# Attention's step list extended over the first two rows of its output product

## The chip, the cores and the metric

The kernel runs on one core of one Trainium2 chip. The metric is the device time of one execution in microseconds (us); before the change the median of three runs is 2084.99 us (2084.24 to 2086.21).

## The reference

Two layers work on x, 1024 tokens by 1024 features in float32. Layer 0 is a gated short convolution and a squared-ReLU MLP; layer 1 is latent attention with shared keys and values and the same kind of MLP. Around each stands a norm, a modulation and a gated sum. The change lies at the end of layer 1's attention:

```python
def mla_mixer(h, q_a_w, q_a_norm_g, q_b_w, o_w, k_nope, v, k_pe, cos, sin):
    q = (rmsnorm(h @ q_a_w, q_a_norm_g) @ q_b_w).reshape(B, S, N_HEADS, QK_NOPE + QK_ROPE)
    ...
    for i in range(S // Q_BLOCK):
        s = (jnp.einsum("bqhd,bkhd->bhqk", qn, k_nope[:, :k_end])
             + jnp.einsum("bqhr,bkr->bhqk", qp, k_pe[:, :k_end])).astype(jnp.float32)
        s = jnp.where(mask[None, None], s, jnp.finfo(jnp.float32).min)
        p = jax.nn.softmax(s, axis=-1).astype(v.dtype)
        outs.append(jnp.einsum("bhqk,bkhd->bqhd", p, v[:, :k_end]))
    o = jnp.concatenate(outs, axis=1).reshape(B, S, N_HEADS * V_HEAD)
    return o @ o_w
```

There are 8 heads of 128 value features. The last line, `o @ o_w`, is the output product: 1024 by 1024 times 1024 by 1024.

## The kernel before

**Precision.** Every large product is made of three matmuls of split operands: a value is kept as a high part (fp32r) and a low part (the rest), and `mm` (L225 to L227) issues low x high, high x low, high x high. The split costs one ScalarE instruction for the high part (L230) and one VectorE instruction for the low part (L231).

**The output product.** `down` (L906) works in rows. Row r holds 128 features of `o` (head r, stored in DRAM as `hd[r]`) and the 128 matching rows of `attn_o_w`, each split into high and low: one `slot` of four 128x1024 pieces. `fill_row` (L802) loads the two raw tiles on SyncE's queue (`ld`, L196) and makes the four pieces: two instructions on ScalarE (L230) and two on VectorE (L231). For each of 8 tiles of 128 tokens, a group of rows is multiplied into a PSUM tile `big` of two banks, of which there are two: 12 matmuls of 512 columns for a group of two rows. The groups are 2, 2 and 4 rows. For the first group ScalarE copies `big` into `y` (L941), for the second VectorE adds it (L943), and the last goes through the norm of the seam.

**Memory.** The raw tiles are a ring of four, shared by all loads. Attention keeps the queries and the rotary keys in slots 0 and 1; slot 2 has held an operand of the stage before and is not used in attention. The pool `pp` holds the shared keys and a cosine table. Before the change all this is released after attention, and six new slots are laid out (`arena_pool`) for the output product.

**Order.** The string `ATTENTION` is a list of steps. `pinned` records each step's instructions so that every engine keeps them in the list's order; SyncE's loads are pinned for the part that belongs to attention. The framework may still place instructions that are outside the list between them. The step names that matter here, for head h: S (scores into `big`), m (maximum, VectorE), e (exponential, ScalarE), t (scaling by the sum, VectorE); for a half of the queries and a group of key tiles: T (transposes into a `tp` PSUM tile), u and w (its high part on ScalarE, L1668, and its low part on VectorE, L1672, both into `pt`), P (product with the values), o (copy out, and store into `hd`). K, Q, R, V are the projections. bl and bs are loads and sums of a modulation vector that fill gaps.

```python
    for name in ATTENTION[n:]:
        acts[name]()
    ...
    at.release()
    tb.release()
    pp.release()
    ar[1].release()
    ...
    ar, slots = arena_pool()
    up, ws, hs, firsts, _ = down_phase(slots, (2, 2, 4), attn_o_w[0], from_dram(hd), "g1m", xs[1], xs[2], ...)
```

Of the kernel before, what the change touches and what calls it, by code (L numbers as in the profile page):

```python
# [66 lines left out]
mm5 mm6 add5 sq5 stt5 xad5 tr0_0 tr0_1 tu0_0 add6 mm7 dma5 tu0_1 rc4 sp0_0 sq6 sp0_1 sqx5 stt6 pre4 rc5 xad6 pre5 tr0_2 f0  # L67
add7 tu0_2 dma6 mul7 sqx6 tr0_3 tr0_4 sp0_2 f1 tu0_3 rc6 sq7 sp0_3 tr0_5 pre6 f2 stt7 tu0_5 tu0_4 sp0_5 dma7 tr0_6 tr0_7
sqx7 sp0_4 f3 tu0_6 rc7 pre7 sp0_6 f4 tu0_7 sp0_7 tr1_0 tr1_1 tu1_0 f5 tu1_1 sp1_0 sp1_1 tr1_2 tr1_3 tu1_2 f6 tu1_3 sp1_2
sp1_3 tr1_4 tr1_5 tu1_4 f7 tu1_5 sp1_4 sp1_5 tr1_6 qh00 tr1_7 g0 qh01 ql00 tu1_7 ql01 tu1_6 sp1_7 qq00 trk0_0 qh02 trk0_1  # L70
sp1_6 g1 tuk0_0 qq01 ql02 tuk0_1 qa01 trk0_2 spk0_0 trk0_3 qq02 g2 spk0_1 tuk0_3 qa02 tuk0_2 spk0_3 trk0_4 trk0_5 qs0 spk0_2
tuk0_5 g3 qr0 spk0_5 tuk0_4 spk0_4 e0 qi0 trk0_6 wa0 trk0_7 e2 qh10 wd0 qq10 tuk0_7 ql10 tuk0_6 spk0_7 trk1_0 qh12 trk1_1 e1
spk0_6 wa2 tuk1_1 ql12 tuk1_0 wd2 trk1_2 spk1_1 qq11 trk1_3 v00 wa1 qa11 tuk1_2 spk1_0 qq12 qh11 spk1_2 tuk1_3 qa12 spk1_3
ql11 trk1_4 wd1 vr00 trk1_5 qs1 tuk1_4 qwa trk1_6 spk1_4 k0 qr1 tuk1_6 qi1 qwd vq00 tuk1_5 spk1_6 spk1_5 trk1_7 v01 kwa
tuk1_7 kwd ka0 spk1_7 kz0 ky0 v11 ks0 vr01 kh0 vq01 kl0 va0 vs0 v10 vt0 vi0 vb0 vr10 k1 vn01 vr11 vn00 vq10 vq11 vh01 va1
vh00 vl01 vl00 vs1 ka1 bB0 R0.1 vt1 kz1 K0.0 Ra0.1 bl0.1 vi1 ky1 bl0.0 vb1 ks1 Q0.1 vn10 lq1 Ka0.0 vn11 vh10 Rz0.1 vh11
Kd0.0 Qa0.1 vl10 K1.0 kh1 Qd0.1 kl1 Q0.0 vl11 Ka1.0 qa1 Ry0.1 Kd1.0 Rs0.1 K0.1 Qa0.0 qd1 Rh0.1.0 Qd0.0 Rh0.1.1 R0.0 Rl0.1.0
Ka0.1 Rl0.1.1 Kd0.1 V0.3 bs0.0 Ra0.0 bs0.1 S0.7 bl0.2 Va0.3 bl0.3 Ry0.0 Rz0.0 S0.4 Vd0.3 Rs0.0 m0.7 V0.2 Rh0.0.0 Rh0.0.1
bs0.2 Q1.1 e0.7 Rl0.0.1 bl0.4 Va0.2 m0.4 S0.5 Qa1.1 t0.7 e0.4 Vd0.2 S0.6 Qd1.1 Rl0.0.0 m0.5 V0.0 m0.6 e0.5 V0.1 Va0.0 t0.4
e0.6 t0.5 S0.1 Vd0.0 Va0.1 S0.2 t0.6 K1.1 m0.1 Vd0.1 e0.1 T0.1.0 m0.2 T0.1.1 Ka1.1 S0.0 u0.1.0 t0.1 Q1.0 u0.1.1 lq2 Kd1.1  # L80
e0.2 w0.1.0 w0.1.1 lk1 T0.1.2 t0.2 Qa1.0 T0.1.3 m0.0 S0.3 u0.1.2 Qd1.0 u0.1.3 e0.0 w0.1.2 P0.1.0 qa2 w0.1.3 P0.1.1 t0.0
T0.1.4 qd2 P0.1.2 u0.1.4 m0.3 S1.4 xa1 w0.1.4 e0.3 xd1 R1.1 m1.4 t0.3 P0.1.3 e1.4 bs0.3 P0.1.4 Ra1.1 T0.1.5 t1.4 T0.1.6
bl0.5 S1.5 bs0.4 u0.1.6 Rz1.1 S1.7 u0.1.5 bl0.6 w0.1.6 w0.1.5 Ry1.1 m1.5 T0.0.0 Q2.1 u0.0.0 m1.7 e1.5 S1.6 w0.0.0 Qa2.1
Rs1.1 e1.7 Qd2.1 bs0.5 Rh1.1.0 T0.0.1 P0.1.5 Rh1.1.1 m1.6 u0.0.1 P0.1.6 bl0.7 P0.0.0 o0.1 T0.0.2 w0.0.1 S1.1 u0.0.2 t1.5
e1.6 K2.0 t1.7 P0.0.1 t1.6 Ka2.0 S1.2 w0.0.2 Kd2.0 P0.0.2 Rl1.1.0 T1.1.0 o0.0 T1.1.1 m1.2 V1.1 u1.1.1 Rl1.1.1 e1.2 w1.1.1
K2.1 u1.1.0 bs0.6 Va1.1 T1.1.2 w1.1.0 Ka2.1 S1.3 u1.1.2 Vd1.1 Kd2.1 T1.1.3 Q2.0 m1.3 u1.1.3 w1.1.3 e1.3 w1.1.2 R1.0 t1.2
Qa2.0 t1.3 Qd2.0 S1.0 bs0.7 Ra1.0 P1.1.0 lq3 P1.1.1 m1.0 m1.1 T1.1.4 T1.1.5 e1.0 P1.1.2 Rz1.0 u1.1.4 P1.1.3 Ry1.0 u1.1.5
w1.1.4 e1.1 S2.4 w1.1.5 qa3 Rs1.0 T1.1.6 qd3 P1.1.4 Rh1.0.1 t1.1 S2.7 Rh1.0.0 m2.4 u1.1.6 Rl1.0.1 e2.4 w1.1.6 t1.0 P1.1.5
m2.7 P1.1.6 Q3.1 o1.1 t2.4 e2.7 Rl1.0.0 S2.6 Qa3.1 t2.7 Qd3.1 K3.1 m2.6 V1.3 Ka3.1 e2.6 Kd3.1 T1.0.0 T1.0.1 Va1.3 t2.6 V1.2
u1.0.0 u1.0.1 Vd1.3 w1.0.0 S2.1 Va1.2 w1.0.1 V1.0 m2.1 Vd1.2 T1.0.2 e2.1 S2.5 u1.0.2 t2.1 Va1.0 w1.0.2 Vd1.0 S2.3 m2.5 bE0  # L90
m2.3 e2.5 e2.3 t2.5 S2.2 t2.3 bB1 bl1.0 bF0 T2.1.0 bl1.1 S2.0 u2.1.0 m2.2 lk2 P1.0.0 lq4 m2.0 P1.0.1 e2.2 w2.1.0 e2.0 P1.0.2
t2.2 T2.1.1 o1.0 K3.0 t2.0 bs1.0 u2.1.1 Q3.0 w2.1.1 Ka3.0 bl1.2 xa2 bs1.1 T2.1.2 Kd3.0 qa4 bl1.3 T2.1.3 xd2 P2.1.0 u2.1.2
# [24 lines left out]
u6.0.1 P6.0.0 t7.6 u6.0.2 e7.0 S7.3 w6.0.1 o6.1 w6.0.2 T7.1.0 t7.0 T7.1.1 m7.3 u7.1.0 P6.0.1 u7.1.1 w7.1.0 S7.1 e7.3 w7.1.1
P6.0.2 T7.1.2 m7.1 o6.0 T7.1.3 P7.1.0 t7.3 u7.1.3 P7.1.1 u7.1.2 w7.1.3 S7.2 e7.1 w7.1.2 T7.1.4 t7.1 T7.1.5 m7.2 u7.1.4
P7.1.2 u7.1.5 w7.1.4 P7.1.3 e7.2 w7.1.5 T7.1.6 P7.1.4 t7.2 u7.1.6 P7.1.5 w7.1.6 T7.0.0 T7.0.1 u7.0.0 P7.1.6 u7.0.1 w7.0.0
o7.1 w7.0.1 T7.0.2 P7.0.0 u7.0.2 P7.0.1 w7.0.2 P7.0.2 o7.0  # L120
""".split()

VEC_ROWS = 109
BIAS_ROWS = 112
C_ID, C_T = 0, 128
WIDE = 64
C_COLS = 2176


@with_exitstack  # L130
def trunk_kernel(ctx: ExitStack, tc: tile.TileContext, x, ada_w, ada_b, norm_g, conv_in_w, conv_out_w, kv_ada_w,
# [676 lines left out]
    def down_pairs(ys, wd, before):  # L808
# [1056 lines left out]
```

## Time and profile before

| | |
|---|---|
| median of three runs | 2084.99 us |
| the profiled execution | 2085.6 us, of which the span on the core is 2083.8 us |
| granted TensorE clock, mean of the span | 0.998 |
| busy share: PE, PE weight load, VectorE, ScalarE | 99%, 82%, 73%, 51% |
| stretch of the latents, from their first steps to the first head | about 997 to 1092 us |
| stretch of attention's heads | about 1092 to 1365 us |
| stretch of the output product's first two groups and of its last group up to the first transposes for the MLP | about 1365 to 1440 us |

PE is TensorE's matmuls, PEld its weight loads, DVE is VectorE, ACT ScalarE, SP SyncE (it only issues loads here). Matmuls are pipelined: a row gives each matmul's own time, which overlaps the next one's, so the time that a group takes is read from the chain of work, where the pieces follow each other. Idle time in brackets, with the instruction that ended it, is the engine's wait.

### The profile page before, as it was taken

What the parts mean: (1) busy time and instruction counts of PE and PEld (TensorE: products, weight loads), DVE (VectorE), ACT (ScalarE), POOL (GpSimd) and SP (SyncE); (2) the same over time, 40 slices, a digit from 0 to 9 for tenths busy, and PEclk for the clock granted to TensorE, in tenths of its full rate; (3) what the DMA queues carried; (4) which work ended last, traced back from release to release, by engine and by line L of the source; (5) the groups of instructions that cost most, each with busy time, mean ns of one, the idle gap of its engine ahead of it and who ended that gap; (6) DMA issues with size and microseconds to landing.
All of it is one profiled execution on the core that took longest, in us unless ns stands there. A gap on an engine that the chain in (4) does not pass through costs nothing.

```text
span 2083.8 us, 25410 instructions
## 1 busy us (share of the span) xinstructions
PE 2061.7 (99%) x9709; PEld 1716.1 (82%) x9709; DVE 1525.3 (73%) x2119; ACT 1058.7 (51%) x1506; POOL 4.6 (0%) x9
## 2 busy tenths in 40 slices
PE   8999999999999999999999999999999999999998
PEld 6888878888888888888888888878888888888887
DVE  7887776977665668876769999767976665559556
ACT  6533264845444533445756566556744454444342
POOL 0000000000000000000000000000000000000000
PEclk9999999999999999999999999999999999999999
DMA  7435464466443976556323232065455544753343
GB/s 284 116 120 151 142 219 136 120 200 210 152 156 119 325 236 229 163 198 199 98 73 87 76 109 88 31 202 162 113 184 173 187 160 178 268 193 111 101 142 142
DMA packets 222450, 330.86 MB, mean 159 GB/s; under 512 B 17268, under 2 KB 121972, under 8 KB 222328
## 3 DMA queue, kind: packets, MB, share of 16 engines
q1 hardware_dynamic: 184744, 248.68, 38.0%
q10 hardware_dynamic: 37584, 80.56, 10.3%
q8 instruction: 76, 1.25, 0.3%
q14 instruction: 46, 0.38, 0.1%
HBM read 248.45 MB, written 80.74 MB: 158 GB/s over the span
## 4 chain that ended last, share of the span: by engine, by line
PE 88%; DVE 7%; DMA 2%; ACT 2%; issue 1%; SPq 0%; DVEq 0%; ACTq 0%
PE one L227 41%; PE mm L227 20%; PE big L227 11%; PE tp L227 7%; PE big L1628 4%; PE tp L1660 1%; PE tp L1345 1%; DMA raw<-in_ada_w_dram 1%; ACT junk L315 1%; DVE y L366 1%; DMA w<-in_conv_first_dram 0%; DMA aw<-in_ada_first_dram 0%; DVE y L370 0%; PE tp L475 0%; DVE raw L345 0%
## 5 line engine op out<-in xcount | busy, mean ns | idle before, releaser
L227 PE MATMUL one<-slot,uphi 128*128 128x512 f32 x1240 | 381.7, 389 | 0.0
L227 PEld LDWEIGHTS one<-slot,uphi 128*128 128x128 f32 x1240 | 232.8, 188 | 48.4 <-issue 0.5
L227 PE MATMUL big<-slot 128*128 128x512 f32 x1152 | 264.1, 390 | 0.7 <-DVE y L1171 0.4
L227 PEld LDWEIGHTS big<-slot 128*128 128x128 f32 x1152 | 215.5, 188 | 45.7 <-ACT y L941 0.8
L227 PE MATMUL one<-slot,uplo 128*128 128x512 f32 x620 | 243.0, 392 | 2.4 <-DVE y L621 1.6
L230 ACT ACTIVATE ring<-w 128x1024 fp32r<-128x1024 f32 x98 | 103.8, 1059 | 260.5 <-PE tp L227 141.9
L227 PE MATMUL one<-ring,ring 128*128 128x512 f32 x1008 | 229.1, 389 | 0.0
L227 PEld LDWEIGHTS one<-ring,ring 128*128 128x128 f32 x1008 | 189.2, 188 | 39.3
L231 DVE TENSOR_TENSOR ring<-w,ring 128x1024 fp32r<-128x1024 f32 x98 | 119.8, 1223 | 116.8 <-ACT ring L230 116.7
L231 DVE TENSOR_TENSOR uplo<-raw,uphi 128x1024 fp32r<-128x1024 f32 x114 | 139.2, 1224 | 78.8 <-ACT uphi L230 78.8
L230 ACT ACTIVATE uphi<-raw 128x1024 fp32r<-128x1024 f32 x114 | 120.6, 1059 | 136.6 <-PE one L227 67.9
L227 PE MATMUL mm<-ring,ring 128*128 128x512 f32 x672 | 162.7, 390 | 1.2 <-DVE ring L231 1.2
L227 PE MATMUL tp<-ring,ring 128*128 128x512 f32 x672 | 161.6, 389 | 0.0
L227 PEld LDWEIGHTS mm<-ring,ring 128*128 128x128 f32 x672 | 125.5, 188 | 28.4 <-DVE ring L231 2.2
L227 PEld LDWEIGHTS tp<-ring,ring 128*128 128x128 f32 x672 | 126.1, 188 | 26.2
L227 PEld LDWEIGHTS one<-slot,uplo 128*128 128x128 f32 x620 | 116.4, 188 | 27.9 <-DVE y L621 2.4
L227 PE MATMUL mm<-slot,uphi 128*128 128x512 f32 x424 | 130.9, 390 | 0.0
L231 DVE TENSOR_TENSOR ring<-raw,ring 128x1024 fp32r<-128x1024 f32 x98 | 119.5, 1219 | 10.8 <-ACT ring L230 10.8
L227 PE MATMUL one<-slot,s 128*128 128x512 f32 x468 | 112.6, 389 | 1.6 <-DVE s L231 1.6
L256 DVE SCALAR_TENSOR_TENSOR acc<-raw,csil,acc 128x1024 f32<-128x1024 f32 x66 | 84.6, 1282 | 36.1 <-DMA raw<-in_ada_w_dram 35.0
L619 ACT ACTIVATE y<-one 128x512 f32<-128x512 f32 x62 | 36.7, 592 | 142.4 <-PE one L227 112.3
L230 ACT ACTIVATE ring<-raw 128x1024 fp32r<-128x1024 f32 x98 | 102.2, 1045 | 4.2 <-DMA raw<-ha 3.8
(291 smaller groups left out, 3509.3 us busy)
## 6 DMA issues: line engine op xcount, KB each, us to landing
ha<-y ACTq DMA_DIRECT2D x196, 256.0 KB, 3.0
raw<-ha SPq DMA_DIRECT2D x98, 512.0 KB, 4.2
raw<-in_ada_w_dram SPq DMA_DIRECT2D x80, 512.0 KB, 4.2
raw<-in_mlp_up_w_dram SPq DMA_DIRECT2D x70, 512.0 KB, 5.1
w<-in_mlp_down_w_dram SPq DMA_DIRECT2D x56, 512.0 KB, 5.1
raw<-hd SPq DMA_DIRECT2D x24, 512.0 KB, 4.5
xs<-raw ACTq DMA_DIRECT2D x24, 512.0 KB, 3.4
raw<-xs SPq DMA_DIRECT2D x24, 512.0 KB, 4.6
```

The lines of the kernel that those rows point to most:

```text
L227: nc.tensor.matmul(out_, lhs[a], rhs[b], start=first and i == 0, stop=last and i == 2, skip_group_check=more)
L230: nc.scalar.activation(hi, src, AF.Copy)
L231: nc.vector.tensor_tensor(lo, src, hi.bitcast(F32), op=ALU.subtract)
L256: nc.vector.scalar_tensor_tensor(acc, raw, s, acc, op0=ALU.mult, op1=ALU.add)
L315: nc.scalar.activation(junk, src, AF.Square, accum_out=ss)
L366: nc.vector.tensor_tensor(y, y, p_, op=ALU.add)
L619: nc.scalar.activation(dst, x_, AF.Copy)
L1345: nc.tensor.transpose(p_[:, t * P:(t + 1) * P], ys[hf * 4 + t][:, k * P:(k + 1) * P], ident)
L1628: nc.tensor.matmul(o_, a, m_, start=j == 0, stop=j == 4)
L1660: nc.tensor.transpose(p_[:, c_:c_ + P], pts[h, 4 * hf + i][:, j * P:(j + 1) * P], ident)
```

## The change

The list goes on past attention. New steps Lw and Ls load the raw tiles of rows 0 to 3 (weights and `hd`), Fa and Fd split a row's weights (ScalarE, VectorE), Fb and Fe split its `hd`, G0 to G7 are the products of rows 0 and 1 for the eight tiles, Ge0 to Ge7 copy them to `y`. Row 0 goes into slot 2, row 1 into a new pool `pre` that takes the place of `pp`, rows 2 and 3 into slots 0 and 1. `down` then begins with row 2 (groups of 2 and 4), and fills rows 4 to 7 itself. The work is the same in number: each engine issues as many compute instructions as before. All the rest of the list, from its first step on, is in another order as well. The lines of the helpers move by one: L196, L227, L230, L231 become L197, L228, L231, L232; the steps' fills are L1747 and L1751, and the copies to `y` L1758.

```diff
+Rh3.1.0 w5.1.2 P5.1.0 Ka6.1 Rl3.1.1 P5.1.1 u5.1.3 Rl3.1.0 T5.1.4 Kd6.1 P5.1.2 u5.1.4 w5.1.3 S5.0 S6.4 w5.1.4 Lw0 m5.0 Ls0
...
+T7.0.2 G2 o7.1 w7.0.1 u7.0.2 w7.0.2 G3 Ge2 P7.0.1 Ge3 P7.0.2 G4 o7.0 G5 Ge4 G6 Ge5 G7 Ge6 Ge7
...
+    def tile_product(t, rows, by_halves=False):
+        p_ = big_ps()
+        ts_ = slice(t * P, (t + 1) * P)
+        parts = [(i, n) for i in range(len(rows)) for n in range(2)]
...
+            mm(p_[:, sl], (s_[:, 2, ts_], s_[:, 3, ts_]), (s_[:, 0, sl], s_[:, 1, sl]), i == 0, i == len(rows) - 1)
+        return p_
...
-                if f >= 3 or not begun:
+                if f >= (4 if f0 else 3) or not begun:
                     fill_row(slot, wd, src_fn, f)
...
+        first_rows(acts)
...
+    def first_rows(acts):
+        raw, p_ = {}, {}
+        def load(r, j):
+            raw[r, j] = raw_tile()
+            ld(raw[r, j], attn_o_w[0][r * P:(r + 1) * P, :] if j == 0 else hd[r])
+        def high(r, j):
+            if r == 1 and not pre:
+                pp.release()
+                pre.append(pool("pre"))
+                first_slots[1] = slots_of(pre[0], 1)[0]
+            nc.scalar.activation(first_slots[r][:, 2 * j, :], raw[r, j], AF.Copy)
+        def low(r, j):
+            s_ = first_slots[r]
+            nc.vector.tensor_tensor(s_[:, 2 * j + 1, :], raw[r, j], s_[:, 2 * j, :].bitcast(F32), op=ALU.subtract)
+        def product(t):
+            p_[t] = tile_product(t, first_slots[:2])
+        def out(t):
+            first_ys.append(row_tile())
+            nc.scalar.activation(first_ys[t], p_[t], AF.Copy)
...
+    pre, first_slots, first_ys = [], [slots[2], None, slots[0], slots[1]], []
...
-    pp.release()
-    ar[1].release()
+    pre[0].release()
...
-    ar, slots = arena_pool()
-    up, ws, hs, firsts, _ = down_phase(slots, (2, 2, 4), attn_o_w[0], from_dram(hd), "g1m", xs[1], xs[2],
-                                      mlp_up_w[1], "1f")
+    arb, old = ar[1], slots
+    ara = pool("arA", "right")
+    ar = [ara, arb, pool("arC")]
+    slots = slots_of(ara, 3)
+    slots = [old[2], slots[2], old[0], old[1], *slots[:2]]
+    up, ws, hs, firsts, _ = down_phase(slots, (2, 4), attn_o_w[0], from_dram(hd), "g1m", xs[1], xs[2], mlp_up_w[1], "1f",
+                                       ys=first_ys, f0=2)
```

**First place: TensorE at the end of the last head.** `tp` are T's transposes, `mm` from `pt` and `v` is P, and `big` from `slot` is the output product. Before, with slot_2000 as row 0 and slot_2001 as row 1:

```order
L227 MATMUL big_2018_11680<-slot_2000_11647 128x512 x5
L1660 MATMUL tp_1984_11577<-cs_76,p_1978_11554 128x128
L1660 MATMUL tp_1984_11577<-cs_76,p_1955_11473 128x128
L1660 MATMUL tp_1985_11582<-cs_76,p_1968_11520 128x128
L1660 MATMUL tp_1985_11582<-cs_76,p_1978_11554 128x128
L1660 MATMUL tp_1985_11582<-cs_76,p_1955_11473 128x128 x2
L227 MATMUL mm_1961_11497<-pt_1982_11567,v_1881_11188 128x256
L227 MATMUL mm_1961_11497<-pt_1983_11568,v_1881_11188 128x256
L227 MATMUL mm_1961_11497<-pt_1982_11567,v_1881_11188 128x256
L227 MATMUL big_2018_11680<-slot_2000_11647 128x512
L227 MATMUL big_2019_11694<-slot_2000_11647 128x512
L227 MATMUL big_2018_11680<-slot_2001_11648 128x512 x3
```

Now, at G1, with slot_953 as row 0 and slot_1899 as row 1; tp_1999 is T7.0.1, the 256-column products are P7.1.6, those with pt_1997 and pt_1998 are P7.0.0:

```order
L228 MATMUL big_1996_11632<-slot_953_6940 128x512 x6
L228 MATMUL big_1996_11632<-slot_1899_11249 128x512 x6
L1663 MATMUL tp_1999_11651<-cs_76,p_1959_11486 128x128
L1663 MATMUL tp_1999_11651<-cs_76,p_1988_11598 128x128
L1663 MATMUL tp_1999_11651<-cs_76,p_1970_11526 128x128 x2
L228 MATMUL mm_1964_11505<-pt_1993_11624,v_1882_11189 128x256
L228 MATMUL mm_1964_11505<-pt_1994_11625,v_1882_11189 128x256
L228 MATMUL mm_1964_11505<-pt_1993_11624,v_1882_11189 128x256
L228 MATMUL mm_2001_11661<-pt_1997_11646,v_1711_10514 128x512
L228 MATMUL mm_2001_11661<-pt_1998_11647,v_1711_10514 128x512
L228 MATMUL mm_2001_11661<-pt_1997_11646,v_1711_10514 128x512
L1663 MATMUL tp_2004_11668<-cs_76,p_1988_11598 128x128
```

Before, the framework put ten matmuls of the output product between the last steps of attention; now whole products stand there, G0 to G3, 48 matmuls ahead of attention's last P.

**Second place: VectorE in the same stretch.** `pt` is a w step, `p` with its own name as input a t step, `slot` the low part of a row's fill. Before:

```order
L1648 TENSOR_SCALAR p_1968_11520<-p_1968_11520,small_1971_11529 128x256
L1633 MEMSET big_1967_11514 64x64
L231 TENSOR_TENSOR slot_2000_11647<-raw_2014_11664,slot_2000_11647 128x1024
L1634 TENSOR_REDUCE small_1973_11537<-big_1967_11514 128x1
L1635 TENSOR_TENSOR small_1973_11537<-small_1973_11537,rsq_88 128x1
L1672 TENSOR_TENSOR pt_1975_11542<-tp_1970_11524,pt_1974_11541 128x512
L1672 TENSOR_TENSOR pt_1977_11548<-tp_1972_11532,pt_1976_11547 128x512
L231 TENSOR_TENSOR slot_2000_11647<-raw_2015_11668,slot_2000_11647 128x1024
L1647 RECIPROCAL small_1981_11564<-small_1979_11555 128x1
L231 TENSOR_TENSOR slot_2001_11648<-raw_2016_11672,slot_2001_11648 128x1024
```

Now; p_1988 is t7.2, pt_1998 is w7.0.0, and the four fills are those of rows 2 and 3:

```order
L1675 TENSOR_TENSOR pt_1981_11563<-tp_1977_11550,pt_1980_11562 128x512
L1751 TENSOR_TENSOR slot_952_6939<-raw_1870_11139,slot_952_6939 128x1024
L1675 TENSOR_TENSOR pt_1986_11583<-tp_1983_11569,pt_1985_11582 128x512
L1650 RECIPROCAL small_1990_11605<-small_1989_11599 128x1
L1651 TENSOR_SCALAR p_1988_11598<-p_1988_11598,small_1990_11605 128x384
L1751 TENSOR_TENSOR slot_952_6939<-raw_1914_11315,slot_952_6939 128x1024
L1751 TENSOR_TENSOR slot_951_6938<-raw_1908_11286,slot_951_6938 128x1024
L1675 TENSOR_TENSOR pt_1994_11625<-tp_1991_11608,pt_1993_11624 128x256
L1751 TENSOR_TENSOR slot_951_6938<-raw_1875_11161,slot_951_6938 128x1024
L1675 TENSOR_TENSOR pt_1998_11647<-tp_1995_11627,pt_1997_11646 128x512
```

The fill of row 0 stood between the last scores and the maximum of them; there is none there now, and the fills of rows 2 and 3 stand between the last w steps.

**Third place: ScalarE after attention.** `y` is the copy out of `big`, `slot` the high part of a fill. Before:

```order
L941 ACTIVATE y_2005_11652<-big_2021_11722 128x1024
L230 ACTIVATE slot_1998_11645<-raw_2038_11920 128x1024
L230 ACTIVATE slot_1998_11645<-raw_2039_11924 128x1024
L941 ACTIVATE y_2006_11653<-big_2022_11736 128x1024
L230 ACTIVATE slot_1999_11646<-raw_2040_11928 128x1024
L230 ACTIVATE slot_1999_11646<-raw_2041_11932 128x1024
L941 ACTIVATE y_2007_11654<-big_2023_11750 128x1024
L941 ACTIVATE y_2008_11655<-big_2024_11764 128x1024
```

Now; y_2015 is Ge4 and y_2020 is Ge7, slot_2021 and slot_2022 are rows 4 and 5, slot_953 is row 6 in the place of row 0:

```order
L1758 ACTIVATE y_2015_11747<-big_2012_11718 128x1024
L231 ACTIVATE slot_2021_11796<-raw_2036_11918 128x1024
L231 ACTIVATE slot_2021_11796<-raw_2037_11922 128x1024
L1758 ACTIVATE y_2017_11762<-big_2014_11734 128x1024
L231 ACTIVATE slot_2022_11797<-raw_2038_11926 128x1024
L231 ACTIVATE slot_2022_11797<-raw_2039_11930 128x1024
L1758 ACTIVATE y_2019_11777<-big_2016_11749 128x1024
L231 ACTIVATE slot_953_6940<-raw_2040_11934 128x1024
L231 ACTIVATE slot_953_6940<-raw_2041_11938 128x1024
L1758 ACTIVATE y_2020_11779<-big_2018_11764 128x1024
```

The fills that are mixed with the copies are now two rows further on (4 to 6 in place of 2 to 5), and one copy, that of the last product, stands behind the two fills of row 6. The loads of row 6 wait for raw tiles that the VectorE fills of row 4 give back.

More of the change, by code (lines that the diff above doesn't have):

```diff
@@ L71 @@
[L71 to L80, printed above, removed]
@@ L904, in down_pairs, with down @@
         return [ara, arb, pool("arC")], first + slots_of(ara, 3)[::-1]
-    def down(slots, sizes, wd, src_fn, ys, seam, per_chunk_bg, before_last=None, begun=False):
-        f = 0
-        nf = sum(sizes)
+    def tile_product(t, rows, by_halves=False):
+        p_ = big_ps()
+        ts_ = slice(t * P, (t + 1) * P)
+        parts = [(i, n) for i in range(len(rows)) for n in range(2)]
+        if by_halves:
+            parts.sort(key=lambda part_: part_[1])
+        for i, n in parts:
+            s_, sl = rows[i], slice(n * HALF, (n + 1) * HALF)
+            mm(p_[:, sl], (s_[:, 2, ts_], s_[:, 3, ts_]), (s_[:, 0, sl], s_[:, 1, sl]), i == 0, i == len(rows) - 1)
+        return p_
+    def down(slots, sizes, wd, src_fn, ys, seam, per_chunk_bg, before_last=None, begun=False, f0=0):
+        f = f0
+        nf = f0 + sum(sizes)
         for n_rows in sizes:
@@ L921, in down, with products @@
                 before_last()
-            def products(t, rows=rows, n_rows=n_rows):
-                p_ = big_ps()
-                ts_ = slice(t * P, (t + 1) * P)
-                parts = [(i, n) for i in range(n_rows) for n in range(2)]
-                if f == nf and seam.last and t == NT - 1:
-                    parts.sort(key=lambda part_: part_[1])
-                ts_ = slice(t * P, (t + 1) * P)
-                for i, n in parts:
-                    s_, sl = rows[i], slice(n * HALF, (n + 1) * HALF)
-                    mm(p_[:, sl], (s_[:, 2, ts_], s_[:, 3, ts_]), (s_[:, 0, sl], s_[:, 1, sl]), i == 0, i == n_rows - 1)
-                return p_
+            def products(t, rows=rows):
+                return tile_product(t, rows, f == nf and seam.last and t == NT - 1)
             seam.products = products
@@ L1200, in trunk_kernel, with down_phase @@
     conv_phase()
-    def down_phase(slots, sizes, wd, src_fn, g, xsrc, xdst, next_w, key, ys=None, pairs=True):
+    def down_phase(slots, sizes, wd, src_fn, g, xsrc, xdst, next_w, key, ys=None, pairs=True, f0=0):
         begun = ys is not None
@@ L1728, in attention @@
         sums(acts, 2, w1, 3 * D, "h1f", 48 + 24)
+    def first_rows(acts):
[17 more added lines that the diff above has]
+            nc.scalar.activation(first_ys[t], p_[t], AF.Copy)
+        for r in range(4):
+            for j, names in enumerate((("Lw", "Fa", "Fd"), ("Ls", "Fb", "Fe"))):
+                for name, f in zip(names, (load, high, low)):
+                    acts[f"{name}{r}"] = lambda f=f, r=r, j=j: f(r, j)
+        for t in range(NT):
+            acts[f"G{t}"] = lambda t=t: product(t)
+            acts[f"Ge{t}"] = lambda t=t: out(t)
     def sums(acts, n, w, col, key, brow=0, g=None, row=None):
```

99 lines of the change are left out of this document (54 added, 45 removed).

## The prediction, made before the run

> **What bounds the kernel now.** I read the page's totals first, then a table of stretches around the change, then TensorE's waits there, then the chain of waits and the engines' own rows at the two places where TensorE waits near the end of attention.
>
> ```profile
> span 2083.8 us, 25410 instructions
> PE 2061.7 (99%) x9709; PEld 1716.1 (82%) x9709; DVE 1525.3 (73%) x2119; ACT 1058.7 (51%) x1506; POOL 4.6 (0%) x9
> core 0: us, PE busy (x) PEld busy (x) DVE busy (x) ACT busy (x) POOL busy (x), PEclk, DMA share, GB/s
> 997.00:1092.00 95.00, 95.00 (x503) 80.17 (x501) 65.18 (x113) 60.51 (x98) 0.95 (x1) 1.00 0.26 79
> 1092.00:1120.00 28.00, 26.99 (x153) 23.32 (x153) 27.25 (x52) 17.71 (x33) 0.00 (x0) 1.00 0.25 71
> 1120.00:1160.00 40.00, 40.00 (x227) 34.68 (x226) 38.71 (x84) 26.38 (x51) 0.00 (x0) 1.00 0.29 85
> 1160.00:1200.00 40.00, 39.92 (x232) 34.21 (x231) 36.52 (x79) 22.96 (x48) 0.00 (x0) 1.00 0.29 91
> 1280.00:1320.00 40.00, 40.00 (x235) 35.41 (x234) 33.23 (x81) 27.19 (x56) 0.00 (x0) 1.00 0.11 40
> 1320.00:1357.00 37.00, 36.03 (x227) 32.14 (x225) 29.72 (x76) 22.43 (x45) 0.00 (x0) 1.00 0.05 17
> 1365.00:1383.00 18.00, 17.66 (x78) 14.28 (x78) 9.63 (x8) 15.13 (x16) 0.00 (x0) 1.00 0.70 236
> 1383.00:1440.00 57.00, 56.95 (x254) 46.96 (x253) 37.33 (x40) 26.91 (x40) 0.00 (x0) 1.00 0.43 142
> ```
>
> TensorE (PE) bounds every stretch. In the rows shown it stands still for 1.01 us at the heads' beginning (28.00 - 26.99), 0.97 us at their end (37.00 - 36.03) and 0.34 us in the output product (18.00 - 17.66), and nearly nowhere else. Its clock is full throughout. VectorE (DVE) is next: 38.71 of 40 us in an early head, 29.72 of 37 at the end. TensorE's waits from 1085 to 1400 us have names:
>
> ```profile
> PE tp L1660 <- DVE pt L1672: 1.1, 1, 1.1
> PE mm L227 <- DVE k L1565: 0.6, 1, 0.6
> PE big L1628 <- ACT p L1642: 0.4, 1, 0.4
> PE big L227 <- ACT y L941: 0.3, 1, 0.3
> ```
>
> These four, 2.4 us together, are all that a better order can win by the waits. Three of them in TensorE's own rows (start, us, what, and the wait):
>
> ```profile
> 1092.67 1.65 PE L227 MATMUL mm<-ckT,w 128*128 128x512 f32 x6 [0.61 <-DVE k L1565]
> 1357.10 0.44 PE L1660 MATMUL tp<-cs,p 128*128 128x128 f32 x2 [1.07 <-DVE pt L1672]
> 1382.12 57.42 PE L227 MATMUL big<-slot 128*128 128x512 f32 x252 [0.34 <-ACT y L941]
> ```
>
> A matmul's own time hides part of a gap, so I also took the distances between the 1657 matmul starts from the first of these rows to the last against the usual pitch of each width: they are 7.6 us longer. That is the most that the change can bring.
>
> The chain of waits shows how the last two arise (start, us, what):
>
> ```profile
> 1350.28 0.36 PE mm L227 x3
> 1350.64 0.87 PE tp L1660 x8
> 1353.46 1.07 ACT slot L230
> 1354.56 1.22 DVE slot L231
> 1355.78 0.48 DVE small L1634
> 1356.36 0.70 DVE pt L1672
> 1357.10 0.44 PE tp L1660 x2
> ...
> 1375.33 4.74 DMA raw<-hd
> 1380.10 1.06 ACT slot L230
> 1381.15 0.92 ACT y L941
> ```
>
> At 1357.10 a transpose waits for a w step (DVE pt), which stood behind the fill of row 0 (DVE slot, 1.22 us). At 1382.12 a product waits for a copy (ACT y), which stood behind a fill (ACT slot) whose raw tile took 4.74 us to load.
>
> **The change part by part.** I cost it on the profiled execution, 2085.6 us with a span of 2083.8 and 1.8 outside it; it is 0.6 above the median of 2084.99, and I carry the differences over to the median.
>
> *Matmuls.* None is removed or added; 96 are moved (G0 to G7). The price of one is that of this row, 2.72 / 12 = 0.227 us:
>
> ```profile
> 878.94 2.72 PE mm L227 x12
> ```
>
> So G is 8 x 2.72 = 21.8 us of TensorE work, the same as before: 0.
>
> *The wait at 1357.10.* The fill that caused it is out of that place. Saved: 1.1 us if nothing takes its place, 0 if as much does; I take 1.1 here and count what takes its place as the next term.
>
> *The fills of rows 2 and 3 between the last w steps.* VectorE, from the end of t7.2: three fills, w7.1.6, w7.0.0.
>
> ```profile
> 1363.53 0.43 DVE L1672 TENSOR_TENSOR pt<-tp,pt 128x256 fp32r<-128x256 f32 x1 [0.56 <-ACT pt L1668]
> 1372.94 2.36 DVE L231 TENSOR_TENSOR slot<-raw,slot 128x1024 fp32r<-128x1024 f32 x2 [1.49 <-ACT slot L230]
> 1374.66 2.01 ACT L230 ACTIVATE slot<-raw 128x1024 fp32r<-128x1024 f32 x2
> 1377.81 1.06 ACT L230 ACTIVATE slot<-raw 128x1024 fp32r<-128x1024 f32 x1 [0.22 <-DMA raw<-in_attn_o_w_dram]
> 1374.19 0.33 SPq L196 DMA_DIRECT2D raw<-in_attn_o_w_dram  x1
> ```
>
> Two fills take 2.36, so this is 3 x 1.18 + 0.43 + 0.70 = 4.7 us. TensorE needs t7.2 for T7.0.0 and w7.0.0 for the second matmul of P7.0.0; between them lie T7.0.0 and T7.0.1 (0.87), G1 (2.72), P7.1.6 (0.36) and one matmul (0.23), 4.2 us. It falls short by up to 0.5, or by nothing if TensorE comes to T7.0.0 a little after t7.2. Bounds 0 and +1.1 (the wait of before); I take +0.3, from the shortfall. Behind w7.0.0 on VectorE are only the last two w steps, which P7.0.1 and P7.0.2 need after 5.4 us of products (G2 and G3). If G1 were not there as cover, it would be 2.7 more.
>
> *The copies behind fills after the list.* From the end of G4, ScalarE runs Ge4, two fills of row 4, Ge5, two of row 5, Ge6, two of row 6, Ge7: with 1.0 for each (a pair of fills takes 2.01; a copy 0.92) Ge6 ends at 7.2. The loads of row 6 wait on SyncE for the VectorE fills of row 4, which follow ScalarE's at about 3.4 and 4.6; by the loads before (4.74 for hd; weights issued at 1374.19, used at 1377.81, 3.6) they land at 7.0 and 9.3. So row 6's fills end at 8.2 and 10.4, and Ge7 at 11.3. TensorE ends G5 to G7 at 8.2, the first tile of rows 2 and 3 at 10.9, and then needs Ge7's bank: a wait of 0.4, against 0.34 now: +0.1, with bounds of -0.3 (gone) and +1 (the loads late by that much more). Behind Ge7 on ScalarE are the fills of row 7 and the split of MLP weights, used 15 us later.
>
> *The loads Lw and Ls.* Eight loads are moved ahead on SyncE. The first stands behind the split of the last kv weights on VectorE, the others behind the sums and splits that free raw tiles; the queries' load for head 7 comes after two of them. In TensorE work, the nearest user is over 10 us behind any of the eight loads, twice the 4.74 above, and the MLP's first loads come at the same point of TensorE's work as before. 0, and up to 1 us (one load found late) without that cover.
>
> *The fills of rows 0 and 1* now lie within heads 5 to 7: four times 1.0 on ScalarE and 1.18 on VectorE (4.7). In 1280 to 1357 us VectorE has 77 - 62.95 = 14 us free. 0 if they fall into it; the slower rival has their price if not.
>
> *The rest of the order.* At 1092.67 (0.6) the same three VectorE steps stand ahead of the one that is waited for as before, and one projection covers it: stays, 0, between -0.6 and +0.6. At the first scores' wait (0.4) one ScalarE step in place of two stands between the maximum and the exponential: -0.2, between -0.4 and +0.4. In the middle heads there are hardly any waits, so a new order can win nothing there by the waits; a lower bound is the hidden part of the 7.6, an upper one a wait of 1.1 in each of two heads. I take 0, the value of the rows with 40.00 of 40.
>
> **Sum:** -1.1 + 0.3 + 0.1 + 0 - 0.2 + 0 = -0.9 us: 2084.7 for an execution like the profiled one, 2084.1 for the median. A measurement of this kernel can tell about 0.2% (4.2 us) from no change, so this counts as no change.
>
> **The rivals.**
>
> *The waits only change place* (the change does not do what it says). Matmuls of the product already stood between attention's last steps:
>
> ```profile
> 1359.06 1.41 PE L227 MATMUL big<-slot 128*128 128x512 f32 x5
> 1361.55 1.31 PE L227 MATMUL big<-slot 128*128 128x512 f32 x5
> ```
>
> With these ten much of the cover was there, and the new waits may take all that is won. Upper values of the two new terms (1.1 and 1.0) against 1.1 saved: +1.0, so 2086.0. For it: fills stand before waited-for steps still. Against: G1 to G3 are 8.2 us of cover that was not there.
>
> *Slower: the fills delay the chain S, m, e, t, T.* Place: heads 5 to 7, where the list has eight VectorE fills and eight ScalarE fills among steps that wait for each other. Price: at 1357.10 one VectorE fill before a w step cost 1.1. Eight times this is 8.8; less the 1.1 saved, +7.7, so 2092.7. It decides from five uncovered fills (5 x 1.1 - 1.1 = 4.4). For it: that fill did cost nearly its whole length. Against it speak the sums of the modulation vector,
>
> ```profile
> L1751 DVE SCALAR_TENSOR_TENSOR acc<-raw,csil,acc 128x1024 f32<-128x1024 f32 x22 | 28.1, 1278 | 0.0
> ```
>
> 22 of them, 1.28 us each, that stand between the same steps in rows with 40.00 of 40 us, and the 14 us that VectorE has free.
>
> *Faster: all waits go.* The hidden gaps go too, as whole products are at hand: between 4.2 and 7.6 gained; the middle, 5.9, gives 2079.1. For it: the 7.6. Against: by the same distances 5.4 of it lie before 1350 us, ahead of any product.
>
> *Faster still: holes in TensorE.* If the weight loads tell how full TensorE is, 1120 to 1160 has 5.3 us of holes in 40, and the 38 matmuls that newly stand ahead of attention's end (48 less 10) could go into such holes: 38 x 0.227 = 8.6, so 2076.4. Against: in 1383 to 1440, where TensorE waits for nothing, the loads are busy for 46.96 of 57 (82%), so 87% in a head (34.68 of 40) is no hole. This is the rule of the Trainium skill, Perfetto Trace Analysis, Identifying the Most-Contended Engine, that the busy share of matmuls doesn't tell how close TensorE is to its roofline and that of the weight loads does; by that rule these holes are real, and the trace disagrees.
>
> **How the numbers follow.** Forecast 0.50 (its own range, 2082.5 to 2086), waits that change place 0.24, slower 0.19, all waits gone 0.05, holes 0.02. The predicted time is 2084.1. Beyond 0.2% lie below 2080.8 the two faster cases, 0.07, above 2089.2 the slower one, 0.19, and between them 0.74. The range goes from 2080.8, which leaves out the faster cases, to 2089.5. All upper bounds at once lie 0.8 + 0.9 + 1.0 + 0.6 + 0.6 + 2.2 = 6.1 above the forecast; the range takes in 5.4 of it, and with it the near end of the slower case. Some 0.19 is left out.
>
> **What would show it right or wrong.** In the profile after: no wait of a transpose for DVE pt near 1357; a wait of up to 0.5 of P on DVE pt at the last head's end; a wait of about 0.4 of a product on the copy ACT y after the eighth product, with a fill and a load of `hd` ahead of it in the chain. TensorE's waits from 1085 to 1400 add up to about 1.5 us in place of 2.4. The forecast is wrong if TensorE waits for DVE or ACT p in heads 5 to 7 by more than 4 us together, or if the distances between its starts shrink by more than that.

## The result and the profile after

The changed kernel takes 2092.31 us (median of 6 runs, 2090.21 to 2094.64) against 2084.61 (6 runs) of the kernel before on the same chip: ratio 1.0037, interval 1.0024 to 1.0050. It is 7.7 us slower. No change was forecast (2084.1, between 2080.8 and 2089.5).

The page after, first and third line:

```profile
span 2092.1 us, 25408 instructions
PE 2063.2 (99%) x9708; PEld 1718.2 (82%) x9709; DVE 1524.7 (73%) x2119; ACT 1058.9 (51%) x1506; POOL 4.6 (0%) x9
```

The engines are as busy as before, and the span is 8.3 us longer (2092.1 against 2083.8). To see where, I cut both traces at the same three places of the program: the first product on `ckT` (the heads begin), the first product of the MLP's up projection after attention, the first product on a ring (the MLP's down projection begins). In these tables the first number is the stretch, the second its length, then each engine's busy time; the last three are TensorE's clock, DMA share and GB/s. Before:

```profile
1088.01:1457.04 369.03, 366.49 (x2020) 315.15 (x2019) 313.47 (x612) 229.52 (x420) 0.00 (x0) 1.00 0.34 107
1457.04:1765.45 308.41, 307.63 (x1372) 254.09 (x1371) 219.49 (x295) 162.97 (x211) 0.96 (x1) 1.00 0.50 162
1765.45:2076.00 310.55, 310.55 (x1369) 256.33 (x1367) 195.61 (x184) 126.77 (x146) 0.00 (x0) 1.00 0.48 164
```

After, with the up projection's end and the down projection's beginning apart:

```profile
1087.67:1455.48 367.81, 365.28 (x2020) 315.46 (x2019) 312.85 (x612) 229.39 (x420) 0.00 (x0) 1.00 0.34 107
1455.48:1764.32 308.84, 308.06 (x1371) 253.73 (x1369) 216.58 (x292) 161.28 (x209) 0.95 (x1) 1.00 0.47 153
1764.32:1771.38 7.06, 0.01 (x1) 0.03 (x1) 1.37 (x2) 2.46 (x3) 0.00 (x0) 0.86 0.90 327
1771.38:1777.00 5.62, 5.62 (x14) 4.16 (x15) 3.86 (x4) 5.40 (x8) 0.00 (x0) 0.57 1.05 389
1777.00:2084.00 307.00, 307.00 (x1354) 253.71 (x1354) 193.12 (x182) 121.14 (x140) 0.00 (x0) 1.00 0.47 161
```

The part that the change is about, heads and output product, became 1.22 us shorter. The loss is 300 us further on, in code that the diff does not touch: TensorE stands still for 7 us between the MLP's up and down projections, and then works 5.6 us at a mean clock of 0.57, in which it starts 14 matmuls where 5.62 / 0.227 would be 25. By the three cuts the sum is exact: -0.34 (start of the heads) - 1.22 + 7.49 (up projection to the first ring, 315.90 against 308.41) + 2.37 (from there to the last matmul's start, 312.75 against 310.38) = 8.3.

The wait has one row in TensorE's list, and its chain names the release:

```profile
1763.72 0.61 PE L228 MATMUL one<-slot,uphi 128*128 128x512 f32 x2
1771.38 3.12 PE L228 MATMUL one<-ring,ring 128*128 128x512 f32 x6 [7.05 <-DVE ring L232]
...
1763.91 0.37 SPq L197 DMA_DIRECT2D w<-in_mlp_down_w_dram  x1
1764.37 0.42 SPq L197 DMA_DIRECT2D raw<-ha  x1
```

```profile
1761.84 2.05 PE one L228 x9
1763.89 0.02 issue
1763.91 0.37 SPq L197
...
1764.37 4.53 DMA raw<-ha
1768.90 0.02 issue
1768.92 1.06 ACT ring L231
...
1770.01 1.24 DVE ring L232
```

SyncE issues the down projection's first weight block (`w`) at 1763.91, 0.4 us before the last matmul of the up projection ends, and the activations (`raw<-ha`) behind it. A ring is a tile in which the split operands are made. Load 4.53, split 1.06 and 1.24: with the issues, TensorE has waited 7.05. Before, the same two loads are out at 1742.34 and 1751.35, 23 and 14 us ahead of the first product on a ring:

```profile
1742.34 0.37 SPq L196 DMA_DIRECT2D w<-in_mlp_down_w_dram  x1
1751.35 0.37 SPq L196 DMA_DIRECT2D raw<-ha  x1
```

The order of the loads is the same; what differs is what the first waits for. SyncE's rows of the two programs as built (before, then after), not of the profile:

```
L196 DMA w_14743<-in_mlp_down_w_dram 128x2x512 [waits DMAHW6_49,DMAHW4_49,DVE_49]
L197 DMA w_14741<-in_mlp_down_w_dram 128x2x512 [waits DMAHW6_49,DVE_49,PE_49]
```

A wait for TensorE is new. The block's place is the same in both programs, bytes 149472 to 153568 of each partition. But the upper pool `arA` held four slots before and holds three now, so `up`, allocated beneath it, moved up by one slot, 16 KB. Before, the place had held one of `up`'s raw tiles, last read by VectorE 249 matmuls ahead of the up projection's end. Now it holds a low half of split weights (`uplo`), which TensorE reads until 3 matmuls before that end.

**My theory** (place): the loss is that one 4-KB block's place; the step list loses nothing. **Rivals:** the heads' order (the prediction's slower case, at nearly the same time, 2092.7), and a late load of the activations for a reason of its own.

### The profile page after: what moved, and what is told of

Same layout as the page of the kernel before. It is cut to its first block, busy times and chain, and to the rows that moved or that the text cites. A ratio compares the mean times of both kernels' runs of the same rounds, so it can differ in the third digit from the quotient of the medians.

```text
span 2092.1 us, 25408 instructions
## 1 busy us (share of the span) xinstructions
PE 2063.2 (99%) x9708; PEld 1718.2 (82%) x9709; DVE 1524.7 (73%) x2119; ACT 1058.9 (51%) x1506; POOL 4.6 (0%) x9
## 4 chain that ended last, share of the span: by engine, by line
PE 87%; DVE 7%; DMA 3%; ACT 2%; issue 1%; SPq 0%; DVEq 0%; ACTq 0%
PE one L228 40%; PE mm L228 20%; PE big L228 11%; PE tp L228 7%; PE big L1631 4%; PE tp L1663 2%; DMA aw<-in_ada_first_dram 1%; PE tp L1348 1%; ACT junk L316 1%; DMA raw<-in_ada_w_dram 1%; DMA w<-in_mlp_up_w_dram 1%; DVE y L367 1%; DVE slot L513 0%; DVE y L371 0%; DVE raw L346 0%
## 5 line engine op out<-in xcount | busy, mean ns | idle before, releaser
L228 PE MATMUL one<-slot,uphi 128*128 128x512 f32 x1240 | 381.8, 389 | 0.0
L228 PEld LDWEIGHTS one<-slot,uphi 128*128 128x128 f32 x1240 | 232.8, 188 | 48.3 <-issue 0.5
L228 PE MATMUL big<-slot 128*128 128x512 f32 x1152 | 264.7, 390 | 1.6 <-DVE y L946 0.7
L228 PEld LDWEIGHTS big<-slot 128*128 128x128 f32 x1152 | 215.4, 188 | 47.0 <-DVE y L946 1.1
L228 PE MATMUL one<-slot,uplo 128*128 128x512 f32 x620 | 243.1, 392 | 1.6 <-DVE y L622 1.6
L228 PE MATMUL one<-ring,ring 128*128 128x512 f32 x1008 | 231.6, 392 | 7.1 <-DVE ring L232 7.1
L231 ACT ACTIVATE ring<-w 128x1024 fp32r<-128x1024 f32 x98 | 103.8, 1059 | 263.5 <-PE tp L228 142.1
L228 PEld LDWEIGHTS one<-ring,ring 128*128 128x128 f32 x1008 | 190.6, 189 | 47.6 <-ACT ring L231 7.4
L232 DVE TENSOR_TENSOR ring<-w,ring 128x1024 fp32r<-128x1024 f32 x98 | 119.9, 1223 | 120.8 <-ACT ring L231 120.7
L232 DVE TENSOR_TENSOR uplo<-raw,uphi 128x1024 fp32r<-128x1024 f32 x114 | 139.3, 1224 | 80.1 <-ACT uphi L231 80.1
L231 ACT ACTIVATE uphi<-raw 128x1024 fp32r<-128x1024 f32 x114 | 120.6, 1059 | 136.8 <-PE one L228 82.7
L228 PE MATMUL mm<-ring,ring 128*128 128x512 f32 x672 | 162.6, 390 | 1.3 <-DVE ring L232 1.3
L228 PE MATMUL tp<-ring,ring 128*128 128x512 f32 x672 | 161.6, 389 | 0.0
L228 PEld LDWEIGHTS mm<-ring,ring 128*128 128x128 f32 x672 | 125.6, 188 | 28.3 <-DVE ring L232 2.1
L228 PEld LDWEIGHTS tp<-ring,ring 128*128 128x128 f32 x672 | 126.1, 188 | 26.2
L228 PEld LDWEIGHTS one<-slot,uplo 128*128 128x128 f32 x620 | 116.4, 188 | 27.2 <-DVE y L622 2.4
L232 DVE TENSOR_TENSOR ring<-raw,ring 128x1024 fp32r<-128x1024 f32 x98 | 119.5, 1219 | 19.0 <-ACT ring L231 19.0
L228 PE MATMUL mm<-slot,uphi 128*128 128x512 f32 x424 | 130.9, 390 | 0.0
L228 PE MATMUL one<-slot,s 128*128 128x512 f32 x468 | 112.6, 389 | 1.1 <-DVE s L232 1.1
L231 ACT ACTIVATE ring<-raw 128x1024 fp32r<-128x1024 f32 x98 | 102.2, 1045 | 15.0 <-DMA raw<-ha 14.5
```

What stands on the lines that cost most here:

```text
L228: nc.tensor.matmul(out_, lhs[a], rhs[b], start=first and i == 0, stop=last and i == 2, skip_group_check=more)
L231: nc.scalar.activation(hi, src, AF.Copy)
L232: nc.vector.tensor_tensor(lo, src, hi.bitcast(F32), op=ALU.subtract)
```

## The experiments

All are timed against the kernel before on the same chip (2083.89 for e1 to e4, 2084.11 for e5 to e7, 2084.16 for e8). Times of different sets come from different chips, so kernels are compared by their ratios. The stretches, cut as above, are of the one profiled execution of each kernel (us; the last one to the last matmul's start):

| kernel | time | ratio, interval | heads, output product | up | down |
|---|---|---|---|---|---|
| before | 2084.61 | 1 | 369.03 | 308.41 | 310.38 |
| after | 2092.31 | 1.0037, 1.0024 to 1.0050 | 367.81 | 315.90 | 312.75 |
| e1_exchange | 2083.89 | 0.9999, 0.9990 to 1.0008 | 366.36 | 308.55 | 310.76 |
| e2_before_layout | 2106.98 | 1.0100, 1.0085 to 1.0116 | 378.58 | 315.79 | 313.16 |
| e3_22 | 2091.14 | 1.0031, 1.0020 to 1.0041 | 366.52 | 313.70 | 312.78 |
| e4_ha_first | 2089.71 | 1.0026, 1.0015 to 1.0036 | 367.29 | 312.98 | 313.33 |
| e5_21 | 2085.93 | 1.0006, 0.9997 to 1.0015 | 367.32 | 310.89 | 310.97 |
| e6_before_layout2 | 2093.68 | 1.0046, 1.0033 to 1.0058 | 368.53 | 315.89 | 312.43 |
| e7_products_last | 2089.00 | 1.0024, 1.0015 to 1.0033 | 373.63 | 308.44 | 310.99 |
| e8_all_early | 2081.94 | 0.9993, 0.9984 to 1.0002 | 366.81 | 308.47 | 310.24 |

### One block elsewhere

The weights of this down projection are loaded in blocks of 4 KB per partition: `ws[i][b]` is block i of quarter b, and the first to be loaded is block 0 of quarter 11. `room` gives the blocks their places in memory.

```diff
...
         room(sd, "21", 1, 4)
+        if exchange:
+            i, b = exchange
+            ws[0]["11"], ws[i][b] = ws[i][b], ws[0]["11"]
...
-    ar, slots = down_pairs(ys, mlp_down_w[1], last)
+    ar, slots = down_pairs(ys, mlp_down_w[1], last, (0, "12"))
```

> The changed kernel, with two 4-KB weight blocks of the second MLP's down projection in exchanged places (block 0 of quarter 11, the first that is loaded, and block 0 of quarter 12). Place theory (the first block lies where a weight tile of the up projection was, which TensorE reads until three matmuls before the end, so its load starts 1 us before TensorE runs dry): the wait of 7.05 us goes, and the 2.5 us at half clock behind it; 2092.3 - 9.7 = 2082.6, between 2081.4 and 2084.2, about 2 us under the kernel before. Heads theory (the slower rival of the prediction: fills delay the chain in heads 5 to 7): nothing changes, 2092. Load theory (the loads of the activations come late for a reason of their own): the wait stays, 2092.

Stretches of this kernel, and below them all that TensorE still waits for ahead of the down projection's first product:

```profile
1085.92:1452.28 366.36, 364.95 (x2020) 315.50 (x2019) 312.91 (x612) 229.35 (x420) 0.00 (x0) 1.00 0.33 106
1452.28:1760.83 308.55, 307.77 (x1372) 254.11 (x1370) 219.54 (x295) 162.99 (x211) 0.95 (x1) 1.00 0.51 164
1760.83:2072.00 311.17, 310.98 (x1369) 256.37 (x1367) 195.72 (x184) 126.82 (x146) 0.00 (x0) 1.00 0.47 164
...
PE one L228 <- DVE ring L232: 0.2, 1, 0.2
```

With the places of two blocks exchanged the kernel is level with the one before, in place of 7.7 us slower; the wait is 0.2 in place of 7.05, and the clock is full. The heads theory and the load theory, both 2092, fall. The 2 us under the kernel before that were expected as well are not seen in the time.

### The layout alone

```diff
-    ar, slots = arena_pool()
+    ara, arb = pool("arA", "right"), pool("arB")
+    ar = [ara, arb, pool("arC")]
+    slots = slots_of(arb, 3) + slots_of(ara, 3)
```

> The kernel before with the six slots as three and three in place of two and four, now with rows 0 and 1 of the output product where they were before, so that its fills start as before. Place theory: no wait at the output product's beginning; a wait of 7.1 us ahead of the second down projection and 2.4 to 2.8 us more at half clock, 2083.9 + 9.7 = 2093.6, between 2092 and 2095.5. Any theory that puts the loss into the list's steps: 2083.9, as the list is that of before.

```profile
1086.97:1455.50 368.53, 366.32 (x2021) 315.12 (x2019) 313.03 (x612) 229.72 (x420) 0.00 (x0) 1.00 0.33 107
1455.50:1771.39 315.89, 307.91 (x1371) 253.78 (x1370) 217.70 (x294) 163.79 (x212) 0.96 (x1) 1.00 0.48 156
...
PE one L227 <- DVE ring L231: 7.2, 1, 7.2
```

2093.68 for 2093.6 expected. The kernel before, its list untouched, gets the same wait and the same stretch (315.89 against 315.90) from the new layout. The place is the cause, shown from both sides.

An earlier try of the same also gave the slots the order that they have in the changed kernel (`[lower[2], upper[2], lower[0], ...]`):

> The kernel before, its step list and its output product untouched, with only the six slots of the second output product laid out as in the changed kernel (three in each of the two pools in place of four and two). Place theory: a wait of about 7 us ahead of the second down projection and about 2.5 us at half clock, 2084.6 + 9.7 = 2094.3, between 2092.5 and 2096. Heads theory: within 2 us of 2084.6, as nothing of the heads is changed. Load theory: within 2 us as well, since the loads stand in the order of before.

It missed by 11 us, through its edit:

```profile
PE one L227 <- DVE ring L231: 7.1, 1, 7.1
PE big L227 <- DVE slot L231: 7.1, 1, 7.1
```

The first wait is the expected one. The second is the output product's beginning: row 1 now had its slot over the tiles of the last head's output (`o`), and in the program as built the first instruction of row 1's fill waits for the stores of `o` and stands behind the fills of rows 2 and 3. The stretch is 9.55 us longer than before (378.58 - 369.03): the wait of 7.1, and some 2.4 that the clock explains, which was at half behind this wait too:

```profile
1376.35 5.30 PE L227 MATMUL big<-slot 128*128 128x512 f32 x12 [7.09 <-DVE slot L231]
...
1376.00:1378.00 2.00, 1.66 (x4) 1.37 (x5) 1.51 (x2) 1.07 (x2) 0.00 (x0) 0.50 0.85 252
...
1380.00:1382.00 2.00, 1.84 (x6) 1.12 (x5) 1.14 (x1) 1.93 (x3) 0.00 (x0) 0.68 0.97 272
```

By the last row half clock ends near 1381.3, 4.9 us after TensorE is back; half of that is 2.5.

### How late is too late

> The changed kernel, with block 0 of quarter 11 in the place of block 0 of quarter 22, whose last earlier reader is 13 matmuls ahead of the end of the up projection instead of 3. Place theory: the load starts 10 x 0.227 = 2.3 us earlier, so the wait is 7.05 - 2.3 = 4.8 us; if the clock still halves behind it (2 to 2.5 us), the time is 2092.3 - 2.3 = 2090.0, between 2088.5 and 2091.5; if a wait of 4.8 us doesn't halve the clock, 2087.6. Heads and load theory: 2092.

> The changed kernel, with block 0 of quarter 11 in the place of block 1 of quarter 21, whose last earlier reader is 25 matmuls ahead of the up projection's end instead of 3. Place theory: the load starts 22 x 0.227 = 5.0 us earlier than in the changed kernel, so the wait is 7.05 - 5.0 = 2.1 us. If the half clock comes from the length of TensorE's idle time (it came behind 7.05, 4.9 and 4.3 us), a wait of 2.1 us may be too short for it: 1.00 granted all through, and 2083.9 + 2.1 = 2086.0, between 2084.5 and 2087.5. If any wait halves the clock, 2088.4. Load theory: the wait stays at 7.

> The changed kernel, with the first load of activations of the second down projection issued ahead of the first weight block on the queue, in place of behind it. Load theory (the activations' load is what comes late, held up behind the weight block): the wait goes, 2082.6. Place theory: the activations land some 10 us earlier, but the weight block lands when it did; its split, 1.06 on ScalarE and 1.22 on VectorE, no longer stands behind that of the activations, which saves at most one of the two pairs, 0.4 to 1.2 us: 2091.1 to 2092.

The first two are the exchange of above with `(0, "22")` and `(1, "21")`; the third swaps the order on the queue for the first pair:

```diff
...
+                    early = which == i == 0 and second
-                    if which in (0, 1, 3, 6):
+                    if which in (0, 1, 3, 6) and not early:
                         get(i, b)
...
                     ld(raw, ha[which][2 * i:2 * i + 2].rearrange("q p m -> p q m"))
+                    if early:
+                        get(i, b)
```

TensorE's wait at that seam, in this order:

```profile
PE one L228 <- DVE ring L232: 4.9, 1, 4.9
...
PE one L228 <- DVE ring L232: 2.5, 2, 2.1
...
PE one L228 <- ACT ring L231: 4.3, 1, 4.3
```

The waits of 4.9 and 2.1 are those worked out from the distance in matmuls (4.8 and 2.1), so the place theory holds in its size too. With the activations loaded first, the wait shrinks by 2.8, more than the 0.4 to 1.2 that I expected: I had kept VectorE's 1.24 in the chain, but TensorE now waits for ScalarE's half alone, and the weight load took 3.58 where the pair's second had taken 4.53. The block stays what TensorE waits for; that the activations stood behind it on the queue was not the main cost.

### The clock behind the wait

The down stretch tells what a wait costs beyond itself: 312.75, 312.78 and 313.33 behind 7.05, 4.9 and 4.3 us, and 312.43 and 313.16 behind the 7.2 and 7.1 of e6 and e2, against 310.38 before and 310.97 behind 2.1. The changed kernel's clock (third column from the end), in steps of 2 us, and below it e5_21's behind its wait of 2.1:

```profile
1766.00:1768.00 2.00, 0.00 (x0) 0.00 (x0) 0.00 (x0) 0.00 (x0) 0.00 (x0) 1.00 1.06 407
1768.00:1770.00 2.00, 0.00 (x0) 0.00 (x0) 0.00 (x0) 1.07 (x2) 0.00 (x0) 0.86 1.02 379
1774.00:1776.00 2.00, 2.00 (x6) 1.53 (x5) 1.24 (x2) 2.00 (x4) 0.00 (x0) 0.50 1.04 384
1776.00:1778.00 2.00, 2.00 (x10) 1.66 (x9) 0.02 (x1) 1.95 (x3) 0.00 (x0) 0.94 1.06 391
...
1764.00:1766.00 2.00, 1.00 (x3) 0.59 (x4) 2.00 (x3) 1.09 (x3) 0.00 (x0) 1.00 1.05 392
1766.00:1768.00 2.00, 2.00 (x10) 1.63 (x9) 1.56 (x3) 2.00 (x3) 0.00 (x0) 1.00 1.05 400
```

All the waits of 4.3 us and more at this place are followed by half clock (matmul starts 0.427 us apart in place of 0.227), the wait of 2.1 is not. The price behind is 2.0 to 3.0 us and doesn't grow with the wait: it is about half of the time for which half clock still runs once TensorE is back (4.9 us, so 2.4, in the changed kernel).

The length of one wait does not settle it, and no threshold is shown. In e7_products_last, further down, the clock is at half for 3.4 us behind waits of 0.16, 0.42, 1.76 and 0.48 us that follow each other within 7 us, and in e2_before_layout for 3.4 us each behind single waits of 1.93 (at 763 us) and 2.40 (at 38 us), the first of them shorter than the 2.1 that left it full. The Trainium skill, TensorE: Matmul & The Clock Gate, in its Part 1 on the HAM clock gate, says that the clock halves after an idle window of about 3.4 us and is full again after a busy one. The traces fit the first behind 4.3 us and more, but not behind these shorter waits, as TensorE was never idle for 3.4 us there; they bear the second out only in that the clock returns, about 4.9 us after TensorE resumed in the changed kernel.

### What covers the last head's end

> The changed kernel with the two blocks exchanged (2083.9), and with the eight products G0 to G7 and their copies behind the last head's end instead of between its steps; the fills stay in the list. Cover theory (the products fill TensorE's waits at the last head's end): by the prediction's step 2.7 us for G1 and 0.3 for what fell short with it, and by the trace of the exchanged kernel, where the scaling t that the last transposes need ends 2.5 us behind the point at which TensorE would come without G0, up to 6 us: 2087 to 2090. If the products cover nothing: 2083.9 within 1.5.

```diff
...
-T7.0.2 G2 o7.1 w7.0.1 u7.0.2 w7.0.2 G3 Ge2 P7.0.1 Ge3 P7.0.2 G4 o7.0 G5 Ge4 G6 Ge5 G7 Ge6 Ge7
...
+T7.0.0 w7.1.6 u7.0.0 Fe2 w7.0.0 T7.0.1 P7.1.6 P7.0.0 u7.0.1 T7.0.2 o7.1 w7.0.1 u7.0.2 w7.0.2 P7.0.1 P7.0.2 o7.0 G0 G1 Ge0 G2 Ge1 G3 Ge2
+G4 Ge3 G5 Ge4 G6 Ge5 G7 Ge6 Ge7
...
```

All other steps keep their order, and the exchange of the first experiment is in. The list takes fewer lines, so `mm` is L222 here. Its waits from 1340 to 1400, and the clock:

```profile
PE tp L1660 <- DVE pt L1672: 1.9, 2, 1.8
PE big L222 <- ACT y L1755: 1.1, 2, 0.6
PE mm L222 <- DVE pt L1672: 0.9, 2, 0.5
...
1362.00:1364.00 2.00, 1.85 (x7) 1.61 (x8) 0.77 (x3) 0.57 (x2) 0.00 (x0) 0.64 1.28 238
1364.00:1366.00 2.00, 2.00 (x10) 1.90 (x9) 0.34 (x1) 0.26 (x1) 0.00 (x0) 0.51 0.74 292
```

2089.0, as expected: 1.0024 of the kernel before, where it was 0.9999 with the products in their places. The stretch of heads and output product grows by 7.3 (373.63 - 366.36) in the profiled execution, which at 2091.17 is the longest of its eleven. The products between the steps do hide waits on VectorE, as the prediction had it: 2.8 us of them (1.9 + 0.9) stand here that e1_exchange doesn't have, against the 2.7 that the prediction gave G1. Of the rest of the 7.3, the copies out of `big` account for 1.1 of waits, and 3.4 us at half clock for up to 1.7; what remains is not shown.

### The whole quarter early

```diff
...
-        room(sl, "12", 0, n)
-        room(sl, "11", n - 5, n)
+        first, then = ("11", "12") if early else ("12", "11")
+        room(sl, first, 0, n)
+        room(sl, then, n - 5, n)
         room(sd, "22", 0, n)
-        room(sd, "11", 0, n - 5)
+        room(sd, then, 0, n - 5)
...
```

> The changed kernel with all seven blocks of quarter 11 in the first places of the lower pool (two slots whose last readers are 98 and 74 matmuls ahead of the up projection's end) and quarter 12 behind them. Place theory: no wait ahead of the second down projection, and nothing over the exchange of one block, as the later blocks had time enough. It also asks once more whether what the step list wins shows in the time when the late block is out of the way: in the traces so far the stretch from the heads' first score weights to the MLP takes 367.1 us with the changed list (five kernels) and 368.8 with the old one (two), 1.7 less, so 2084.0 - 1.7 = 2082.3, between 2080.5 and 2084.0. If the later blocks count too, under 2081.

2081.94, the fastest kernel here: 0.9993 of the kernel before, where the changed kernel was 1.0037, and with 1 just inside the interval. So the list's gain shows in the traces (six kernels with it take 366.36 to 367.81 for heads and output product, mean 367.0; two with the old list 369.03 and 368.53, mean 368.8: 1.8 us) but too small for the times to settle.

## Why the prediction was wrong, point by point

**The step that failed** is the list of parts. It costed the matmuls, fills, copies and loads that the list moves, and said of the rest that the MLP's first loads come at the same point of TensorE's work as before, 0 to 1 us. That holds for the up projection, not for the down projection behind it. The slots' new split (three and three) stood in the diff as lines without an instruction, and had no term; what it moved is the memory under everything allocated later. It cost 7.49 us in the up projection's stretch (the wait) and 2.37 in the next (the half clock). The new wait on TensorE in SyncE's row could have been read ahead of the run, but I compared order and counts there, not waits, past the end of attention. The signs of being wrong that the prediction named did not come either (more than 4 us of waits in heads 5 to 7): the loss lay outside the stretch that it watched.

**The slower rival** had the number (2092.7) for a reason that is not there: in the stretch 1320 to 1357, where it put the loss, TensorE now waits for nothing, with VectorE busier than before (32.31 against 29.72):

```profile
1320.00:1357.00 37.00, 37.00 (x225) 32.92 (x224) 32.31 (x81) 25.10 (x50) 0.00 (x0) 1.00 0.13 44
```

**The terms of the sum** were about right. TensorE's waits from 1085 to 1400 after:

```profile
PE big L228 <- DVE y L946: 0.7, 1, 0.7
PE big L1631 <- ACT p L1645: 0.7, 2, 0.5
PE mm L228 <- DVE k L1568: 0.6, 1, 0.6
PE big L228 <- ACT y L1758: 0.5, 1, 0.5
```

- The wait at 1357.10 is gone (-1.1, as said), and none took its place at P7.0.0 (0 for +0.3).
- The wait for Ge7's copy is 0.5 (0.4 said). A wait of 0.7 for the next group's sums (`DVE y`) was not foreseen; e1, e3 and e8, with the same list, don't have it, so it is no fixed part of the list; what sets it is not shown.
- The wait at 1092.67 stays at 0.6. The first scores' wait is 0.7 in two places, where 0.2 in one was said: the term had the wrong sign.
- Together: waits of 2.5 in place of 1.5 said and 2.4 before, yet the stretch is 1.22 shorter here and 1.8 in the mean, against 0.9 forecast. So the gain did not come from the waits, and that the total came near the forecast is luck. It must lie in gaps that no wait row shows, part of the 7.6 us of start distances that the prediction counted as the most to be had; which steps closed them is not shown.

**Holes in TensorE** were not there: with the products among the last heads' steps, the stretch of heads and output product is 1.22 us shorter, not 8.6.

## What to carry to other kernels

A change of pools can change the waits of every load behind it. Where a diff changes how many tiles a pool holds, look at the first load of each later phase and at what its place held last: a list of each load's waits, old against new, shows it without a run. Where TensorE goes from one phase to the next without a pause, put the blocks that are loaded first where the phase before is through earliest; one exchanged pair of blocks was worth the whole 7.7 us here.

## What was not expected of the hardware

A wait of TensorE has a price beyond itself when the clock halves behind it: 2.0 to 3.0 us more behind 4.3 to 7.2 us, 0.6 or less behind 2.1 (310.97 against 310.38). Several short waits close together can bring it too, as in e7_products_last. Half clock lasted, by the 2-us steps, 6.8 us in the changed kernel (0.56 + 3 x 2 + 0.24, twice the missing share of each step).
